# Stores of the feed-forward blocks and the gates issued by the engines that make the data, the residual fetched in four parts, and x ahead of p at the start

## The chip, the cores and the metric

The kernel runs on one core of a Trainium2 chip. A core has five engines that run side by side and wait for each other through semaphores: TensorE (PE, matrix products; its weight loads are listed as PEld), VectorE (DVE), ScalarE (ACT), GpSimd (POOL) and SyncE (SP), which here only issues DMA transfers. The metric is the device time of the whole program in microseconds (us), the median of several runs. Times inside a run are counted from the start of the profiled span.

## What is computed

The reference is one block of an encoder with 1024 tokens of width 1024, in float32:

```
h = x + 0.5 * swiglu(rms_norm(x, g1), Wg1, Wu1, Wd1)      # FFN1, inner width 2816
u = rms_norm(h, g_mix);  z = u @ w_in                     # queries, keys, values, gates
y_a = attention over the 256 best keys of a learned index
y_r = group_norm(chunkwise retention) * silu(rg)
h = h + (sigmoid(ga) * (y_a @ Wa) + sigmoid(gb) * (y_r @ Wb)) @ w_out
h = h + 0.5 * swiglu(rms_norm(h, g2), Wg2, Wu2, Wd2)      # FFN2
h = h + sigmoid(rms_norm(h, g_ple) @ Wpg) * (p @ Wpp)     # per-layer embedding
out = rms_norm(h, g_final)

swiglu(x, Wg, Wu, Wd) = (silu(x @ Wg) * (x @ Wu)) @ Wd
```

## The kernel before

Every float32 operand of a product is split into a high part (a rounded copy, made by ACT at L144 or L401) and a low part (the difference, made by DVE at L146 or L402, or by POOL for some weights), and each product is three matmuls of 128x128 by 128x512 (`split3`).

**Weights.** The class `Weights` holds one list of loads and one list of fills for the whole program. A load takes one of four raw buffers of 512 KB and is a DMA on SP (L155, L172) or a sum or difference made from two raw buffers by POOL (L184, L185, L192, L193). A fill splits a raw buffer into one of four pairs of tiles `wh`, `wl`. `pump` starts a load as soon as a raw buffer is free in the program's order, and a fill as soon as a pair is free. So a load of the next block waits, on SP, for the split that last read its buffer.

**Each FFN** (class `Seven`) uses a form of Strassen's method with seven products in place of eight, in two stages. In `products`, 11 periods (j = 0 to 10) each make the block of 256 inner columns: seven products for the gate matrix, seven for the up matrix (12 matmuls each, `term`, L565), evacuated by ACT (L576, L602) and DVE (L580, L605) into four tiles `h` of 128x512. PE begins to accumulate onto a bank again as soon as ACT has copied it (L576). At the end of a period POOL makes four sums of the four tiles (L627 to L630), and SP stores the seven resulting blocks to DRAM, 256 KB each (`hsp`, L633). Then `down_factors` loads four pieces of the down matrix through SP (L645), POOL forms four differences in place (L646 to L649) and SP stores them (`wsp`, L651): eleven stores a period. In `down`, seven runs of 11 jobs of 12 matmuls (L663) multiply these blocks; each job's raw buffer is filled by two loads of 256 KB, one from `hsp`, one from the down matrix or `wsp`. DVE adds the sums onto the residual `hres` (L672), of which all 16 pieces of 256 KB are fetched before the first run, in FFN1 from x (L796), in FFN2 from `h2spill` (L1548).

**Other stores.** The projection of p (L759) is stored by SP to `ppspill` (L760) while the first norms run; the 24 gate tiles of two halves each are made by ACT (L1036), for the retention gate multiplied by POOL (L1038), and stored by SP (`gspill`, L1039), through two tiles `gt`.

**Order.** The order of PE's instructions is the order of the program text. On the other engines the framework's planner orders the instructions by its own estimate of when each is ready; the engine then works strictly in that order. A DMA on SP whose data or buffer is not ready therefore holds up every DMA behind it.

Of the kernel before, what the change touches and what calls it, by code (L numbers as in the profile page):

```python
# [20 lines left out]
P = 128  # L21
S = 1024
D = 1024
# [254 lines left out]
def hybrid_block_kernel(  # L278
# [27 lines left out]

    LEFT = ["A11", "A12", "S2", "S1", "S3", "S4", "A22"]
    NJ2 = NF // 2  # L310
    hsp, wsp = {}, {}

    def seven_jobs(name, wg, wu, wd):
        hsp[name] = [dram.tile([P, 7, 512], F32, name=f"h{name}{j}") for j in range(NJ2)]
        wsp[name] = [dram.tile([P, 4, 512], F32, name=f"w{name}{j}") for j in range(NJ2)]
        for j in range(NJ2):
            for m, w in (("g", wg), ("u", wu)):
                if (m, j) == ("u", 0):
                    W.early = len(W.fills)
                W.matrix((name, m, j), *(krows(w, 2 * P * j, 2 * P * (j + 1), 4 * q, 4 * q + 4) for q in range(2)))  # L320
        n = W.early
        W.fills[n - 1], W.fills[n] = W.fills[n], W.fills[n - 1]
        for a in LEFT:
            for j in range(NJ2):
                q = LEFT.index(a)
                t = {"S1": 0, "S2": 1, "S3": 2, "A22": 3}.get(a)
                if t is None:
                    f, c = {"A11": (0, 0), "A12": (1, 0), "S4": (1, 512)}[a]
                    wap = krows(wd, c, c + 512, 2 * j + f, 2 * j + f + 1)
                else:  # L330
                    wap = wsp[name][j][:, t:t + 1]
                W.plain((name, a, j), 1, D, False, [(0, 512, hsp[name][j][:, q:q + 1]), (512, D, wap)])
# [150 lines left out]
    class Seven:  # L483
# [66 lines left out]
        def products(self, between):  # L550
# [5 lines left out]
                     "A22": (uh[:, 0:4, b], ul[:, 0:4, b])}  # L556
            left = ExitStack()
            ev = left.enter_context(tc.tile_pool(name="hid", bufs=1))
            g = {0: [ev.tile([P, 512], F32, name=f"g{i}") for i in range(4)]}

            def term(ps, key, start, stop):
                (wh, wl), (bh, bl) = W[key], right[key[1]]
# [42 lines left out]
                return lambda n, t: nc.vector.tensor_tensor(to[n], to[n], t, op=OP.mult)  # L605

            for j in range(NJ2):
                h = g[j % 2]
                gate, up = blocks("g", j, silu(h)), None
                if j == 0:  # L610
                    up = blocks("u", j, times(h))
                    next(gate)
                    next(up)
                    for f in between():
                        f()
                for _ in gate:
                    pass
                if j == 0:
                    self.top.close()
                    sp = self.top.enter_context(tc.tile_pool(name="hid2", bufs=1, side="right"))  # L620
                    g[1] = [sp.tile([P, 512], F32, name=f"g{i}") for i in range(4)]
                for _ in up or blocks("u", j, times(h)):
                    pass
                s1, s2, s4 = (sp.tile([P, 512], F32, name=f"s{i}", tag="s", bufs=8) for i in range(3))
                gp = nc.gpsimd
                h11, h12, h21, h22 = h
                gp.tensor_tensor(s1, h12, h22, op=OP.add)  # L627
                gp.tensor_tensor(s2, s1, h11, op=OP.subtract)
                gp.tensor_tensor(h12, h11, h12, op=OP.subtract)
                gp.tensor_tensor(s4, h21, s2, op=OP.subtract)  # L630
                made = dict(A11=h11, A12=h21, S2=s2, S1=s1, S3=h12, S4=s4, A22=h22)
                for q, n in enumerate(LEFT):
                    nc.sync.dma_start(hsp[self.name][j][:, q], made[n])  # L633
                self.down_factors(sp, j)
            left.close()
            self.top.close()
            self.low.close()

        def down_factors(self, pool, j):

            gp = nc.gpsimd
            b11, b12, b21, b22 = t = [pool.tile([P, 512], F32, name=f"wd{i}", tag="s", bufs=8) for i in range(4)]
            for i in range(4):
                c0 = 512 * (i % 2)
                nc.sync.dma_start(t[i], krows(self.wd, c0, c0 + 512, 2 * j + i // 2, 2 * j + i // 2 + 1)[:, 0])  # L645
            gp.tensor_tensor(b11, b12, b11, op=OP.subtract)  # L646
            gp.tensor_tensor(b12, b22, b12, op=OP.subtract)  # L647
            gp.tensor_tensor(b22, b22, b11, op=OP.subtract)  # L648
            gp.tensor_tensor(b21, b21, b22, op=OP.subtract)  # L649
            for q, d in enumerate((b11, b22, b12, b21)):  # L650
                nc.sync.dma_start(wsp[self.name][j][:, q], d)  # L651

        def down(self, hres, finished, turn, other={}):
            bank_plan(mm=3, m1=1, dn=4)
            sums = [bank(t, "pda") for t in ("mm", "mm", "mm", "m1")]

            def run(a, ps, start, stop, between=None):
                for j in range(NJ2):
                    key = self.name, a, j
                    h, l = (x[:, 0] for x in W[key])  # L660
                    for i in range(4):
                        for n, (x_, y_) in enumerate(split3(h[:, tok(i)], l[:, tok(i)], h[:, 512:D], l[:, 512:D])):
                            nc.tensor.matmul(ps[i], x_, y_, start=start and j == 0 and n == 0,  # L663
                                             stop=stop and j == NJ2 - 1 and n == 2, skip_group_check=True)
                    W.release(key)
                    if between and between.get(j):
                        between[j]()

            def to(ps, t, i):
                for n in range(4):  # L670
                    r = hres[:, 4 * t + n, half(i)]
                    nc.vector.scalar_tensor_tensor(r, ps[n], 0.5, r, op0=OP.mult, op1=OP.add)  # L672

            run("A11", sums, True, False)
            to(sums, 0, 0)
            pc = [bank("dn", "pdc") for _ in range(4)]
            run("A12", pc, True, True)
            to(pc, 0, 0)
            run("S2", sums, False, False)
            to(sums, 0, 1)  # L680
            pc = [bank("dn", "pdc") for _ in range(4)]
            run("S1", pc, True, False)
            to(pc, 1, 1)
            run("S3", sums, False, False)
            to(sums, 1, 1)
            run("S4", pc, False, True)
            to(pc, 0, 1)
            bank_plan(mm=3, m1=1, dn=2, tr=2)
            finished(0)
            finished(1)  # L690

            def turn_and_next(b):
                def go():
                    turn(b)()
                    if b < 2:
                        finished(b + 2)
                return go

            run("A22", sums, False, True, {1 + 2 * b + (b > 1): turn_and_next(b) for b in range(4)} | other)
            to(sums, 1, 0)  # L700
            finished(4)
            finished(5)
# [16 lines left out]
    def load_x(b):  # L719
        nc.sync.dma_start(seven.block(b), x0[tok(b), :])  # L720

    order = [b + 4 * e for b in range(4) for e in range(2)]
    W.limit = 2
    W.load()
    load_p(0)
    seven.open()
    for b in order[:2]:
        load_x(b)
    seven.load_gain()
    W.load()  # L730
    load_p(2)
    for b in order[2:4]:
        load_x(b)
    nc.vector.memset(mhalf, -0.5)
    make_identity(nc, ident)
    W.limit = len(W.loads)
# [17 lines left out]
    def proj_p(b, i):  # L754
        c = slice(P * (b % 2), P * (b % 2) + P)
        th, tl = pt[b & ~1]
        ps = product(("pp", i), b, 2, (lambda k: th[:, k, c], lambda k: tl[:, k, c]))
        t = pk.tile([P, 512], F32, name="ppt", tag="ppt", bufs=2)
        nc.scalar.activation(t, ps, AF.Copy)  # L759
        nc.sync.dma_start(ppspill[:, b, half(i)], t)  # L760

    turns = []
    for i in range(4):
# [27 lines left out]
    ffn1 = ExitStack()  # L791
    hpool = ffn1.enter_context(tc.tile_pool(name="hres1", bufs=1))
    hres = hpool.tile([P, NB, D], F32, name="hres")
    for i in range(2):
        for b in range(NB):
            nc.sync.dma_start(hres[:, b, half(i)], x0[tok(b), half(i)])  # L796
    nc.sync.dma_start(cs, cst)


# [53 lines left out]
            f()  # L853

    finished = normed(mix_norm[0], hres, hspill)
    seven.down(hres, finished, turn, {4: lambda: W.drop(raws)})
    for b in range(2):
        for j in range(2):
            sm_product(2 * b + j, "dn")
# [161 lines left out]
    def gate_half(c, f, i):  # L1021
        box = []

        def piece(k):
# [11 lines left out]
            nc.scalar.activation(t, box[0], AF.Copy if raw else AF.Silu if c == RG else AF.Sigmoid)  # L1036
            if c == RG:
                nc.gpsimd.tensor_tensor(t, t, gnt[:, f:f + 1].to_broadcast([P, 512]), op=OP.mult)  # L1038
            nc.sync.dma_start(gspill[c][:, f, half(i)], t)  # L1039

        return [lambda k=k: piece(k) for k in range(KT)]

# [500 lines left out]
    rpool = late.enter_context(tc.tile_pool(name="res", bufs=1))  # L1543
    hres = rpool.tile([P, NB, D], F32, name="hres2")
    npool = late.enter_context(tc.tile_pool(name="norm2", bufs=1))
    for i in range(2):
        for b in range(NB):
            nc.sync.dma_start(hres[:, b, half(i)], h2spill[:, b, half(i)])  # L1548
    gl = {}

    def ple_gate(b, i=0, parts=1, tag="mm"):
# [7 lines left out]
        return fs + [done]  # L1559

    finished = normed(ple_norm[0], hres)
    seven.down(hres, finished, turn)


    ph = ExitStack()
# [82 lines left out]
```

## Time and profile before

| | us |
|---|---|
| median of three runs (2648.21 to 2649.6) | 2648.36 |
| the profiled execution | 2651.99 |
| its span | 2650.2 |
| PE busy in the span | 2489.3 (94%) |
| DVE, ACT, POOL busy | 1514.1, 1100.8, 899.4 |

The stages by their place in the span: start to 66 us (norm of x, projection of p, first transposes), `products` of FFN1 to 532, `down` of FFN1 to 763, index scores to 925, retention and selection to 1300, attention to 1606, merge and output product to 1874, `products` of FFN2 to 2322, `down` of FFN2 to 2555, and the embedding with the last norm to the end.

To read it: PE's busy time is the sum of the spans of its matmuls; what is left of the span is the time in which PE waited, and the view of waits says for whom. PEclk is the granted clock of TensorE, 1.00 being 2.4 GHz and 0.50 being 1.2 GHz; a mean between the two in a stretch says for which part of it the lower one held. Each other view has its columns named where its rows stand.

### The profile page before, as it was taken

What the parts mean: (1) busy time and instruction counts of PE and PEld (TensorE: products, weight loads), DVE (VectorE), ACT (ScalarE), POOL (GpSimd) and SP (SyncE); (2) the same over time, 40 slices, a digit from 0 to 9 for tenths busy, and PEclk for the clock granted to TensorE, in tenths of its full rate; (3) what the DMA queues carried; (4) which work ended last, traced back from release to release, by engine and by line L of the source; (5) the groups of instructions that cost most, each with busy time, mean ns of one, the idle gap of its engine ahead of it and who ended that gap; (6) DMA issues with size and microseconds to landing.
All of it is one profiled execution on the core that took longest, in us unless ns stands there. A gap on an engine that the chain in (4) does not pass through costs nothing. (4 is left out here: it accounts for less than half of the span.)

```text
span 2650.2 us, 32857 instructions
## 1 busy us (share of the span) xinstructions
PE 2489.3 (94%) x11464; PEld 2030.7 (77%) x11464; DVE 1514.1 (57%) x2640; ACT 1100.8 (42%) x1900; POOL 899.4 (34%) x688
## 2 busy tenths in 40 slices
PE   6999999989999998989999999998999999989998
PEld 5777777768888777767878887787777777768887
DVE  5444444455567879997457664635444444445564
ACT  5333333334355667652235653414323233334452
POOL 5356565410000333343443431004456565410000
PEclk8999999989999999989999999999999999989999
DMA  5244344576640221221221218642244444586632
GB/s 194 92 135 158 130 146 139 172 261 212 192 155 21 84 81 33 68 80 44 86 82 37 82 61 244 183 161 82 94 133 147 130 156 138 174 296 203 196 98 95
DMA packets 272230, 349.36 MB, mean 132 GB/s; under 512 B 22976, under 2 KB 152256, under 8 KB 272064
## 3 DMA queue, kind: packets, MB, share of 16 engines
q1 hardware_dynamic: 272064, 347.27, 41.3%
q8 instruction: 90, 1.47, 0.2%
q14 instruction: 76, 0.62, 0.1%
HBM read 246.00 MB, written 101.19 MB: 131 GB/s over the span
## 5 line engine op out<-in xcount | busy, mean ns | idle before, releaser
L146 DVE TENSOR_TENSOR wl<-wraw,wh 128x1024 fp32r<-128x1024 f32 (+2 forms) x422 | 521.0, 1241 | 542.9 <-ACT wh L144 528.2
L144 ACT ACTIVATE wh<-wraw 128x1024 fp32r<-128x1024 f32 (+1 forms) x466 | 436.5, 938 | 852.1 <-PE pc L565 195.1
L439 PE MATMUL prod<-wh,uh 128*128 128x512 f32 (+1 forms) x648 | 266.6, 411 | 0.2 <-ACT gt L1036 0.2
L439 PE MATMUL prod<-wh,ul 128*128 128x512 f32 (+1 forms) x648 | 257.8, 398 | 0.0
L439 PE MATMUL prod<-wl,uh 128*128 128x512 f32 (+1 forms) x648 | 257.3, 397 | 0.0
L565 PE MATMUL pa<-th,wh 128*128 128x512 f32 x352 | 142.8, 406 | 43.2 <-ACT ev L576 43.2
L1029 PE MATMUL pgate<-uh,wh 128*128 128x512 f32 x384 | 159.2, 415 | 20.9 <-ACT gt L1036 19.8
L663 PE MATMUL pda<-wh 128*128 128x512 f32 x352 | 140.3, 399 | 21.4 <-ACT wh L144 10.7
L465 POOL TENSOR_TENSOR nst<-nst,mhalf 128x1 f32<-128x1 f32 x16 | 8.7, 550 | 443.6 <-DVE nst L464 443.6
L1029 PE MATMUL pgate<-uh,wl 128*128 128x512 f32 x384 | 154.5, 402 | 0.0
L1029 PE MATMUL pgate<-ul,wh 128*128 128x512 f32 x384 | 154.4, 402 | 0.0
L439 PEld LDWEIGHTS prod<-wh,ul 128*128 128x128 f32 x648 | 123.7, 191 | 29.2
L565 PE MATMUL pa<-ul,wh 128*128 128x512 f32 x352 | 141.2, 401 | 4.7 <-DVE ul L402 4.7
L1096 ACT ACTIVATE bias<-bias 128x1024 bf16<-128x1024 bf16 (+3 forms) x132 | 117.3, 890 | 63.0 <-DVE bias L1095 61.7
L146 POOL TENSOR_TENSOR wl<-wraw,wh 128x1024 fp32r<-128x1024 f32 x44 | 109.7, 2496 | 98.5 <-ACT wh L144 97.9
L565 PE MATMUL pa<-th,wl 128*128 128x512 f32 x352 | 142.7, 405 | 0.0
L565 PE MATMUL pa<-uh,wh 128*128 128x512 f32 x352 | 140.6, 399 | 1.8 <-ACT uh L401 1.8
L565 PE MATMUL pa<-tl,wh 128*128 128x512 f32 x352 | 142.0, 403 | 0.0
L663 PE MATMUL pda<-wl,wh 128*128 128x512 f32 x352 | 139.5, 396 | 2.5 <-DVE wl L146 2.5
L565 PE MATMUL pa<-uh,wl 128*128 128x512 f32 x352 | 140.8, 400 | 0.0
L565 PE MATMUL pc<-uh,wl 128*128 128x512 f32 x352 | 139.7, 397 | 0.0
L565 PE MATMUL pc<-ul,wh 128*128 128x512 f32 x352 | 139.6, 396 | 0.0
(274 smaller groups left out, 6008.0 us busy)
## 6 DMA issues: line engine op xcount, KB each, us to landing
wraw<-hf SPq DMA_DIRECT2D x154, 256.0 KB, 3.0
wraw<-in_ffn_w_gate_dram SPq DMA_DIRECT2D x44, 512.0 KB, 5.2
wraw<-in_ffn_w_up_dram SPq DMA_DIRECT2D x44, 512.0 KB, 3.8
hf<-g SPq DMA_DIRECT2D x88, 256.0 KB, 2.3
wd<-in_ffn_w_down_dram SPq DMA_DIRECT2D x88, 256.0 KB, 4.3
wf<-wd SPq DMA_DIRECT2D x88, 256.0 KB, 2.6
wraw<-wf SPq DMA_DIRECT2D x88, 256.0 KB, 3.2
hf<-s SPq DMA_DIRECT2D x66, 256.0 KB, 2.0
```

The costliest lines, as they stand in the source:

```text
L144: self.nc.scalar.activation(h, src, AF.Copy)
L146: eng.tensor_tensor(l, src, h.bitcast(F32), op=OP.subtract)
L439: nc.tensor.matmul(box[0][:, :cols], a, w, start=k == 0 and i == 0, stop=k == nk - 1 and i == 2)
L465: nc.gpsimd.tensor_tensor(st[:, 1:2], st[:, 0:1], mhalf, op=OP.pow)
L565: nc.tensor.matmul(ps, x_, y_, start=start and k == 0 and i == 0, stop=stop and k == 3 and i == 2, skip_group_check=True)
L663: nc.tensor.matmul(ps[i], x_, y_, start=start and j == 0 and n == 0, stop=stop and j == NJ2 - 1 and n == 2, skip_group_check=True)
L1029: nc.tensor.matmul(box[0], a, m, start=k == 0 and j == 0, stop=k == KT - 1 and j == 2)
L1096: nc.scalar.activation(m, m, AF.Copy, accum_out=cnt[:, j:j + 1])
```

## The change

- `products`: the four tiles `h` become one tile of 128x4x512. The seven stores of a period become three, issued by POOL (`nc.gpsimd`): one of 1 MB (`h`, four blocks side by side in DRAM), one of 512 KB (S2 and S1), one of 256 KB (S4). The order of the blocks in DRAM follows (`HID`).
- `down_rows`: the four loads of down-matrix pieces are issued by SP ahead of the up products of the same period, into two tiles of 128x2x2x256; `down_factors` then makes eight differences of 128x256 on POOL and two stores of 512 KB, issued by POOL. The tag `s` has five buffers of 512 KB (it had eight of 256 KB), of which a period takes four.
- `down`: the residual is not fetched before the first run, but in four parts of four pieces, at the fifth job of the runs A11, A12, S2 and S1. A one-column copy on POOL from that job's weights into each piece holds its DMA back until then.
- The stores of the projection of p, and of the gates ga and gb, are issued by ACT; those of the retention gate by POOL.
- At the start p's first load comes first, then one weight load, x's first two blocks and the gain, the second weight load, x's next two blocks, p's second load.

```diff
@@ products
-            g = {0: [ev.tile([P, 512], F32, name=f"g{i}") for i in range(4)]}
+            g = {0: ev.tile([P, 4, 512], F32, name="g0")}
...
+                wd = self.down_rows(sp, j)
                 for _ in up or blocks("u", j, times(h)):
                     pass
-                s1, s2, s4 = (sp.tile([P, 512], F32, name=f"s{i}", tag="s", bufs=8) for i in range(3))
+                sa, sb = (sp.tile([P, 2, 512], F32, name=f"s{i}", tag="s", bufs=5) for i in range(2))
+                s2, s1, s4 = sa[:, 0], sa[:, 1], sb[:, 0]
...
-                for q, n in enumerate(LEFT):
-                    nc.sync.dma_start(hsp[self.name][j][:, q], made[n])
-                self.down_factors(sp, j)
+                to = hsp[self.name][j]
+                gp.dma_start(to[:, 0:4], g[j % 2])
+                gp.dma_start(to[:, 4:6], sa)
+                gp.dma_start(to[:, 6], s4)
+                self.down_factors(wd, j)
@@ down factors
+        def down_rows(self, pool, j):
+            wd = [pool.tile([P, 2, 2, 256], F32, name=f"wd{i}", tag="s", bufs=5) for i in range(2)]
+            for q in range(2):
+                for f in range(2):
+                    rows = krows(self.wd, 0, D, 2 * j + f, 2 * j + f + 1)[:, 0].rearrange("p (i c) -> p i c", i=2)
+                    nc.sync.dma_start(wd[q][:, f], rows[:, :, 256 * q:256 * q + 256])
+            return wd
...
+            for q in range(2):
+                b11, b12, b21, b22 = (wd[q][:, i // 2, i % 2] for i in range(4))
...
+                gp.dma_start(wsp[self.name][j][:, :, 256 * q:256 * q + 256],
+                             wd[q].rearrange("p f i c -> p (f i) c"))
@@ down
+            def fetch(t, i):
+                def go(h):
+                    for b in range(4 * t, 4 * t + 4):
+                        nc.gpsimd.tensor_copy(hres[:, b, 512 * i:512 * i + 1], h[:, 0:1].bitcast(F32))
+                        nc.sync.dma_start(hres[:, b, half(i)], residual(b, i))
+                return go
...
+                    if load and j == 4:
+                        load(h)
...
+            run("A11", sums, True, False, load=fetch(0, 0))
+            run("A12", pc, True, True, load=fetch(0, 1))
+            run("S2", sums, False, False, load=fetch(1, 1))
+            run("S1", pc, True, False, load=fetch(1, 0))
...
-    for i in range(2):
-        for b in range(NB):
-            nc.sync.dma_start(hres[:, b, half(i)], x0[tok(b), half(i)])
@@ projection of p, gates
-        nc.sync.dma_start(ppspill[:, b, half(i)], t)
+        nc.scalar.dma_start(ppspill[:, b, half(i)], t)
...
-            nc.sync.dma_start(gspill[c][:, f, half(i)], t)
+            (nc.gpsimd if c == RG else nc.scalar).dma_start(gspill[c][:, f, half(i)], t)
```

## Rows read from the trace of the kernel before

**Rows 1.** Waits of PE over the whole span: us in total, times, longest us.
```profile
PE pa L565 <- ACT ev L576: 43.2, 18, 4.2
PE pgate L1029 <- ACT gt L1036: 19.8, 8, 4.5
```

**Rows 2.** Timeline of PE: start us, us, what, idle before it and its releaser.
```profile
225.39 0.51 PE L565 MATMUL pa<-th,wh 128*128 128x512 f32 x1 [2.65 <-ACT ev L576]
```

**Rows 3.** Timelines of ACT and DVE in the same period and the half before.
```profile
190.61 1.22 DVE L146 TENSOR_TENSOR wl<-wraw,wh 128x1024 fp32r<-128x1024 f32 x1 [3.31 <-ACT wh L144]
...
209.76 1.23 DVE L146 TENSOR_TENSOR wl<-wraw,wh 128x1024 fp32r<-128x1024 f32 x1 [4.53 <-ACT wh L144]
...
223.21 0.63 ACT L144 ACTIVATE wh<-wraw 128x512 fp32r<-128x512 f32 x1 [7.41 <-DMA wraw<-in_ffn_w_gate_dram]
```

**Rows 4.** Timeline of SP's queue, 180 to 226 us: time of issue, length, transfer, count.
```profile
191.91 0.37 SPq L172 DMA_DIRECT2D wraw<-in_ffn_w_up_dram  x1
...
206.42 0.32 SPq L633 DMA_DIRECT2D hf<-s  x1
...
208.76 0.38 SPq L172 DMA_DIRECT2D wraw<-in_ffn_w_gate_dram  x1
213.42 5.30 SPq L651 DMA_DIRECT2D wf<-wd  x4
218.81 0.39 SPq L172 DMA_DIRECT2D wraw<-in_ffn_w_gate_dram  x1
```

**Rows 5.** Windows of `products`: length, busy us of each engine, PEclk, DMA share, GB/s.
```profile
66.00:532.00 466.00, 440.29 (x1867) 353.80 (x1867) 209.09 (x227) 150.84 (x228) 245.34 (x164) 0.98 0.43 139
...
220.00:260.00 40.00, 37.35 (x155) 29.90 (x154) 18.67 (x20) 13.23 (x20) 21.53 (x15) 0.96 0.42 138
...
1930.00:1970.00 40.00, 39.57 (x159) 31.91 (x160) 17.81 (x20) 11.49 (x17) 22.55 (x15) 0.92 0.43 141
```

**Rows 6.** Windows of the two handovers from `products` to `down`.
```profile
532.00:572.00 40.00, 29.34 (x123) 22.48 (x121) 11.13 (x11) 7.31 (x7) 12.78 (x8) 0.94 0.83 282
572.00:596.00 24.00, 21.73 (x81) 17.37 (x82) 22.81 (x41) 13.07 (x15) 0.00 (x0) 0.81 0.71 230
...
573.00:583.00 10.00, 8.73 (x23) 6.60 (x24) 9.93 (x17) 5.96 (x6) 0.00 (x0) 0.59 0.77 243
...
2322.00:2345.00 23.00, 11.96 (x49) 9.23 (x48) 4.71 (x5) 4.55 (x5) 10.49 (x8) 0.79 0.82 273
...
2343.00:2353.00 10.00, 9.31 (x29) 7.14 (x30) 5.86 (x6) 5.30 (x7) 0.00 (x0) 0.69 0.92 296
```

**Rows 7.** Timelines of SP and PE in the handovers.
```profile
555.49 10.41 SPq L796 DMA_DIRECT2D hres<-in_x_dram  x16
...
566.92 0.33 SPq L155 DMA_DIRECT2D wraw<-in_ffn_w_down_dram  x1
...
573.71 0.80 PE L663 MATMUL pda<-wh 128*128 128x512 f32 x1 [9.37 <-ACT wh L144]
...
2336.68 3.00 SPq L651 DMA_DIRECT2D wf<-wd  x3
```

**Rows 8.** Timeline of ACT at a gate; SP's gate stores: duration ns min/median/max, first and last start us.
```profile
1005.36 1.28 ACT L1036 ACT_TABLE_LOAD   x1
...
L1039 SPq DMA_DIRECT2D gspill<-gt x48: 319/336/1311, 847.2 to 1613.1; - x48
```

**Rows 9.** POOL: one line (ns min/median/max), then groups by shape (busy us, mean ns | idle).
```profile
L649 POOL TENSOR_TENSOR wd<-wd,wd x22: 1262/2151/2261, 133.6 to 2338.1; 128x512 f32<-128x512 f32 x22
...
L1214 POOL TENSOR_TENSOR sl<-sf,sh 128x256 fp32r<-128x256 f32 x28 | 21.7, 777 | 18.0 <-ACT sh L1213 18.0
...
L465 POOL TENSOR_TENSOR nst<-nst,mhalf 128x1 f32<-128x1 f32 x16 | 8.7, 550 | 443.6 <-DVE nst L464 443.6
```

**Rows 10.** The page's DMA issues: count, KB each, median us to landing.
```profile
wf<-wd SPq DMA_DIRECT2D x88, 256.0 KB, 2.6
```

**Rows 11.** Window of the start.
```profile
0.00:66.00 66.00, 45.29 (x204) 35.21 (x204) 34.71 (x48) 36.58 (x65) 34.02 (x35) 0.90 0.57 195
```

More of the change, by code (lines that the diff above doesn't have):

```diff
@@ L302, in tile_job @@
         W.plain(key, nk, n * P, side, [(0, n * P, krows(w, f * P, (f + n) * P, 0, nk))])
+    HID = ["A11", "S3", "A12", "A22", "S2", "S1", "S4"]
     LEFT = ["A11", "A12", "S2", "S1", "S3", "S4", "A22"]
@@ L324, in seven_jobs @@
             for j in range(NJ2):
-                q = LEFT.index(a)
-                t = {"S1": 0, "S2": 1, "S3": 2, "A22": 3}.get(a)
+                q = HID.index(a)
+                t = {"S1": 0, "S3": 1, "A22": 2, "S2": 3}.get(a)
                 if t is None:
@@ L607, in products @@
             for j in range(NJ2):
-                h = g[j % 2]
+                h = [g[j % 2][:, i] for i in range(4)]
                 gate, up = blocks("g", j, silu(h)), None
@@ L620, in products @@
                     sp = self.top.enter_context(tc.tile_pool(name="hid2", bufs=1, side="right"))
-                    g[1] = [sp.tile([P, 512], F32, name=f"g{i}") for i in range(4)]
+                    g[1] = sp.tile([P, 4, 512], F32, name="g1")
+                wd = self.down_rows(sp, j)
                 for _ in up or blocks("u", j, times(h)):
                     pass
-                s1, s2, s4 = (sp.tile([P, 512], F32, name=f"s{i}", tag="s", bufs=8) for i in range(3))
+                sa, sb = (sp.tile([P, 2, 512], F32, name=f"s{i}", tag="s", bufs=5) for i in range(2))
+                s2, s1, s4 = sa[:, 0], sa[:, 1], sb[:, 0]
                 gp = nc.gpsimd
@@ L630, in products @@
                 gp.tensor_tensor(s4, h21, s2, op=OP.subtract)
-                made = dict(A11=h11, A12=h21, S2=s2, S1=s1, S3=h12, S4=s4, A22=h22)
-                for q, n in enumerate(LEFT):
-                    nc.sync.dma_start(hsp[self.name][j][:, q], made[n])
-                self.down_factors(sp, j)
+                to = hsp[self.name][j]
[3 more added lines that the diff above has]
+                self.down_factors(wd, j)
             left.close()
@@ L637, in products @@
             self.low.close()
-        def down_factors(self, pool, j):
-            gp = nc.gpsimd
[L642 to L651, printed above, removed]
@@ L653, in down, with down_factors @@
-        def down(self, hres, finished, turn, other={}):
+        def down_rows(self, pool, j):
[5 more added lines that the diff above has]
+            return wd
+        def down_factors(self, wd, j):
+            gp = nc.gpsimd
+            for q in range(2):
+                b11, b12, b21, b22 = (wd[q][:, i // 2, i % 2] for i in range(4))
+                gp.tensor_tensor(b11, b12, b11, op=OP.subtract)
+                gp.tensor_tensor(b12, b22, b12, op=OP.subtract)
+                gp.tensor_tensor(b22, b22, b11, op=OP.subtract)
+                gp.tensor_tensor(b21, b21, b22, op=OP.subtract)
+                gp.dma_start(wsp[self.name][j][:, :, 256 * q:256 * q + 256],
+                             wd[q].rearrange("p f i c -> p (f i) c"))
@@ L654, in down, with run @@
+        def down(self, hres, residual, finished, turn, other={}):
             bank_plan(mm=3, m1=1, dn=4)
             sums = [bank(t, "pda") for t in ("mm", "mm", "mm", "m1")]
-            def run(a, ps, start, stop, between=None):
+            def fetch(t, i):
[4 more added lines that the diff above has]
+                return go
+            def run(a, ps, start, stop, between=None, load=None):
@@ L672, in to @@
                     nc.vector.scalar_tensor_tensor(r, ps[n], 0.5, r, op0=OP.mult, op1=OP.add)
-            run("A11", sums, True, False)
+            run("A11", sums, True, False, load=fetch(0, 0))
             to(sums, 0, 0)
             pc = [bank("dn", "pdc") for _ in range(4)]
-            run("A12", pc, True, True)
+            run("A12", pc, True, True, load=fetch(0, 1))
             to(pc, 0, 0)
-            run("S2", sums, False, False)
+            run("S2", sums, False, False, load=fetch(1, 1))
             to(sums, 0, 1)
             pc = [bank("dn", "pdc") for _ in range(4)]
-            run("S1", pc, True, False)
+            run("S1", pc, True, False, load=fetch(1, 0))
             to(pc, 1, 1)
@@ L722, in hybrid_block_kernel @@
     order = [b + 4 * e for b in range(4) for e in range(2)]
+    seven.open()
+    load_p(0)
+    W.limit = 1
+    W.load()
+    load_x(order[0])
+    load_x(order[1])
+    seven.load_gain()
     W.limit = 2
     W.load()
[L725 to L731, printed above, removed]
     for b in order[2:4]:
         load_x(b)
+    load_p(2)
     nc.vector.memset(mhalf, -0.5)
@@ L855, in hybrid_block_kernel @@
     finished = normed(mix_norm[0], hres, hspill)
-    seven.down(hres, finished, turn, {4: lambda: W.drop(raws)})
+    seven.down(hres, lambda b, i: x0[tok(b), half(i)], finished, turn, {4: lambda: W.drop(raws)})
     for b in range(2):
@@ L1545, in hybrid_block_kernel @@
     npool = late.enter_context(tc.tile_pool(name="norm2", bufs=1))
-    for i in range(2):
-        for b in range(NB):
-            nc.sync.dma_start(hres[:, b, half(i)], h2spill[:, b, half(i)])
     gl = {}
@@ L1561, in hybrid_block_kernel @@
     finished = normed(ple_norm[0], hres)
-    seven.down(hres, finished, turn)
+    seven.down(hres, lambda b, i: h2spill[:, b, half(i)], finished, turn)
     ph = ExitStack()
```

## The prediction

> **What bounds the kernel now.** I read the page's shares first: PE is busy in 2489.3 of 2650.2 us, so what can be won without taking products away is the 161 us in which it waits, and stretches at the lower clock. Then the waits of PE [rows 1]. The largest is 43.2 us in 18 pieces: a matmul of `products` waits until ACT has copied its bank (L576). ACT is far from full, so the question is what ACT waits for, and the timelines of one period answer it. PE stands for 2.65 us until 225.39 [rows 2]; ACT stood from 215.8 to 223.21, 7.41 us, for the second load of the next gate matrix, and the copy that PE needs is queued behind that split [rows 3]. SP issued this load at 218.81, directly behind the four stores of the down factors, which held SP from 213.42 to 218.72 while POOL made their data [rows 4]. The buffer it loads into had been free since DVE's split of 209.76 ended, 210.99 [rows 3]: the load was 7.8 us late. The other half of the period is the control: there the load at 191.91 follows its split (190.61 + 1.22 = 191.83) at once [rows 3, 4], and no wait of PE follows. The 18 waits lie in 18 different periods of the 22.
>
> The second place is the handover from `products` to `down`. PE is idle 40 - 29.34 = 10.7 and 24 - 21.73 = 2.3 us in FFN1, and 23 - 11.96 = 11.0 us in FFN2 [rows 6]. In FFN1 SP spends 555.49 to 566 on 16 loads of the residual, the next weight load goes out at 566.92, and PE stands 9.37 us until 573.71; in FFN2 SP is held by the last factor stores until 2339.7 [rows 7].
>
> **The change, part by part.**
>
> *Stores of `products` to POOL.* Eleven stores of some 0.33 us and all their waits for POOL leave SP; its queue in the loop keeps loads alone. The late load can go out at about 211, lands before 216, and ACT's split stands ready when a pair of tiles comes free. So the 43.2 us go, and with them what the clock loses after them: in five stretches of 40 us of the two loops (one is shown) the mean granted clock is 0.96, in one 0.92 [rows 5], that is the 1.2 GHz level for 3.2 us and 6.4 us of the stretch, a loss of 5 x 1.6 + 3.2 = 11.2 us. Together 54.4 us. I take 80%: the control half shows that a load in time ends the wait, but the 1 MB store now leaves in one piece beside these loads, and the loads of the down rows sit in SP's queue ahead of the up products, and one of the two buffers they need comes free only when a factor store of the period before has landed. That is 43.5 us off the path.
>
> *What POOL pays.* POOL is busy 245.34 us in 11 periods of FFN1, 22.3 a period [rows 5]. Four differences of 128x512 become eight of 128x256: 8 x 0.777 [rows 9] against some 6.0, +0.3 at most. The five stores have no row: no DMA is issued by POOL in this trace. From below they cost what SP's cost, 0.34 each [rows 8]; a gain is excluded, since POOL issues none now. From above, POOL would be held until the data has landed: 2.6 us for 256 KB [rows 10], for 2.75 MB a period eleven times that, 28.6, or 5.7 a store. I take 1.0: a POOL instruction with almost no data takes 0.55 [rows 9], a store needs no arithmetic on the data, and SP is released long before its data lands. So 22.6 + 5 = 27.6 us of POOL in a period that without waits lasts (466 - 25.7 - 4.8)/11 = 39.6 us [rows 5]: hidden. Behind POOL's stores stand the weight sums of the next matrix; POOL no longer waits for the down rows, which come half a period ahead, and that gives about as much time back.
> A POOL difference beside a DVE split of two SBUF operands takes 2.15 instead of 1.26 us [rows 9], so a store might be stretched by 0.9 us as well, 4.5 us a period, still hidden. The Trainium skill's page "SBUF — State Buffer", section "Who interferes with whom", agrees for arithmetic (a DVE instruction with two SBUF inputs contends with POOL's reads), but infers that writing a DMA's descriptors is not held up by it; by that the 4.5 us would be 0, and the sum is the same either way.
>
> *Handovers.* The stores and waits leave SP here too, and the residual goes out in fours of 256 KB, the first at the fifth job of A11. What can be won: FFN1 12.9 us idle and, after it, 10 us at a mean clock of 0.59, which loses 4.1; FFN2 11.0 and 10 us at 0.69, 3.1 [rows 6]; 31.1 together. I take 65%, 20.2 us: the last period's chain on POOL stays, the DMA engines are 0.82 to 0.92 busy there, and the first quarter of the residual is issued behind POOL's last stores (about 553), lands some 6 us later, and is needed by DVE when A11 ends at 532 + 11 jobs x 12 x 0.227 = 562.
>
> *Gates.* PE's 19.8 us for the gates [rows 1] are not SP's doing: ACT comes late because its own queue is full and a table load of 1.28 us stands before the gate [rows 8]. Nothing is won. 32 stores of 0.34 us [rows 8] come onto ACT, 10.9 us, beside PE's products; behind each stands ACT's next evacuation. I add 1 us (0 to 4). POOL's 16 fall where it is mostly idle.
>
> *Start.* 16 stores of 0.34, 5.4 us, come onto ACT, which is busy 36.6 of 66 us in a chain of short steps [rows 11]; SP, freed of them, loads x earlier; x's second pair goes out half a microsecond sooner. I add 0.7 (-4 to +4).
>
> Sum: -43.5 - 20.2 + 1 + 0.7 = -62.0. The profiled execution took 2651.99 us for its span of 2650.2; the median of the runs is 2648.36, and the difference is taken from that: 2586 us.
>
> **The rivals.**
> 1. *The handovers keep their time*: for it, the DMA engines are 0.82 to 0.92 busy [rows 6], and the same bytes must move; against it, PE stood while SP was held, not while data was on its way. 2648.4 - 43.5 + 1.7 = 2607.
> 2. *SP is held at another place*: the loads of the down rows wait in SP's queue for buffers that POOL's stores free, and the late weight load stands behind them as it stood behind the stores. Five buffers and four taken a period speak for it; that these loads come half a period after those stores speaks against it. The loops keep their 54.4: 2648.4 - 20.2 + 1.7 = 2630.
> 3. *Only issue time is saved*: 242 stores x 0.33 = 80 us of SP's queue, none of it on the path, if each load is late for its own buffer. The 7.8 us between a free buffer and its load speak against it. 2648. The Trainium skill's page "DMA: Bandwidth & Descriptors", section "Issuing engines are not separate DMA queues", speaks for it: starting DMAs from several engines saves only the sequencer's time, usually a small part. The trace differs: what holds SP is the wait for data in an ordered queue.
> 4. *POOL becomes the bound*: with c us for a store a period of POOL is 22.6 + 5c. It reaches PE's 39.6 at c = 3.4, and the whole change loses from c = 4.1 on (22 x (22.6 + 5c - 42.4) = 20). For it: the upper end of 5.7, and two of the stores have rows of 1 KB. At c = 4.5: 22 x 2.7 - 20 = +39, 2688.
>
> **How the numbers follow.** Forecast 55%, rival 1 15%, rival 2 14%, rival 3 6%, rival 4 10%. A measurement of this kernel can tell 0.2%, 5 us, from no change. Faster: 55 + 15 + 14 = 84%; same 6%; slower 10%. Low end: all of 54.4 and 31.1 and the start's 4, 2559, a little below it 2556. High end 2644, which takes in rival 2 and leaves rivals 3 and 4 out.
>
> **What would show it.** Right: no stores in SP's queue in the loops, the gate load within 2 us of its split, PE's wait for L576 under 10 us, no weight load of `down` behind 10 us of residual loads, the gates' wait of some 20 us unchanged. Wrong: POOL stores above 3.4 us, or SP waiting for the buffers of the down rows. The forecast fails if PE's waits in `products` merely change their releaser from ACT's late split to POOL's sums.

## The result, and the profile after

The changed kernel takes 2580.01 us (median of 4 runs, 2576.72 to 2586.53) where the kernel before takes 2648.28 beside it (4 runs, 2644.49 to 2649.6): a ratio of 0.9748, 95% interval 0.9726 to 0.9769. The forecast was 2586, 62 us less than before; 68 came. The profiled execution has a span of 2578.6 us, 71.6 less than before.

First the page's shares of the changed kernel (busy us, share of the span, instructions):

```profile
PE 2471.9 (96%) x11464; PEld 2020.6 (78%) x11464; DVE 1604.5 (62%) x2640; ACT 1104.9 (43%) x1900; POOL 1011.1 (39%) x934
```

PE's idle time fell from 161 us to 106.7, and its busy time by 17.4: the products are the same, but fewer of them run at the lower clock (the mean granted clock of FFN1's loop goes from 0.98 [rows 5] to 0.99, below). Then PE's waits in the changed kernel (us in total, times, longest), against [rows 1]:

```profile
PE pgate L1047 <- ACT gt L1054: 21.7, 9, 5.0
...
PE pda L683 <- ACT wh L144: 4.5, 2, 2.3
```

The 43.2 us for ACT's copy of the products' banks are gone from PE's waits without a rest; the gates' wait is as it was (19.8 before). For ACT's split at the handovers PE waits 4.5 us in two pieces; FFN1's alone had one of 9.37 [rows 7].

Where the time went is told best by stages. Each boundary is the first matmul into a tile: `pa`, `pda`, `pgate`, `pmrg`, the second FFN's `pa` and `pda`; the last stage goes to the end of the span. The experiments below are in the same table (us, each from its one profiled execution; the first stage varies by 5 us, so smaller differences carry nothing):

| kernel | start | products 1 | down 1, index | retention, attention | merge | products 2 | down 2, end |
|---|---|---|---|---|---|---|---|
| before | 67.6 | 464.9 | 305.4 | 768.4 | 247.5 | 467.8 | 328.6 |
| after | 66.7 | 442.1 | 292.3 | 770.5 | 247.2 | 440.0 | 319.8 |
| e1_stores_only | 66.0 | 438.4 | 295.4 | 768.0 | 246.1 | 441.4 | 320.0 |
| e2_residual_only | 69.1 | 468.6 | 293.0 | 767.2 | 249.5 | 467.8 | 327.4 |
| e3_issued_by_sp | 64.4 | 507.5 | 294.9 | 769.5 | 249.4 | 503.5 | 321.0 |
| e4_rows_late | 64.6 | 461.6 | 295.8 | 771.6 | 248.2 | 459.4 | 328.7 |
| e5_small_back | 68.4 | 439.7 | 290.8 | 767.4 | 247.3 | 440.9 | 321.0 |
| e6_pool_2_chain | 65.1 | 458.8 | 292.4 | 773.3 | 248.3 | 475.3 | 321.0 |
| e7_pool_2_early | 64.6 | 441.3 | 293.8 | 769.0 | 251.0 | 440.5 | 320.1 |
| e8_raw_gates | 64.5 | 441.9 | 292.3 | 768.3 | 247.7 | 440.9 | 319.5 |

Two loops of products give 22.8 and 27.8 us, two handovers 13.1 and 8.8; the rest is within 2.1.

Windows of the changed kernel that answer to [rows 5, 6]: first the loop of FFN1, 40 us of it and 40 of FFN2's, then the two handovers (length, busy us of PE, PEld, DVE, ACT, POOL, then PEclk, DMA share, GB/s):

```profile
66.70:508.80 442.10, 435.25 (x1869) 350.78 (x1870) 251.57 (x227) 150.56 (x225) 295.40 (x266) 0.99 0.45 151
200.00:240.00 40.00, 39.75 (x172) 31.87 (x171) 24.18 (x20) 13.34 (x20) 28.41 (x26) 1.00 0.45 152
1900.00:1940.00 40.00, 39.78 (x172) 31.89 (x171) 24.40 (x21) 13.34 (x20) 27.96 (x25) 1.00 0.45 152
508.80:548.80 40.00, 36.90 (x156) 29.87 (x155) 28.56 (x47) 16.54 (x18) 11.77 (x15) 0.96 0.82 265
2258.80:2281.80 23.00, 20.10 (x80) 15.85 (x79) 8.54 (x8) 7.71 (x8) 11.13 (x11) 0.93 0.80 283
```

PE is nearly without a gap in the loops, 0.2 us idle in each 40, at a mean granted clock of 0.99 or 1.00. At the handovers its idle time is 3.1 us (it was 10.7) and 2.9 (11.0), while the DMA engines are about as busy as before, 0.82 and 0.80 (0.83 and 0.82 in [rows 6]): the bytes still move, and PE no longer stands for them. Two columns have grown: POOL from 245.34 to 295.40, and DVE from 209.09 to 251.57, although DVE does nothing new. That is the surprise of this case, taken up below.

SP's queue in one period (against [rows 4]), then the two splits that its last gate load stands between, DVE's that frees the buffer and ACT's that needs the data:

```profile
189.02 0.37 SPq L172 DMA_DIRECT2D wraw<-in_ffn_w_up_dram  x1
189.49 1.21 SPq L648 DMA_DIRECT2D wd<-in_ffn_w_down_dram  x2
202.64 0.38 SPq L172 DMA_DIRECT2D wraw<-in_ffn_w_gate_dram  x1
203.12 1.21 SPq L648 DMA_DIRECT2D wd<-in_ffn_w_down_dram  x2
211.48 0.38 SPq L172 DMA_DIRECT2D wraw<-in_ffn_w_gate_dram  x1
```

```profile
207.22 4.17 DVE L146 TENSOR_TENSOR wl<-wraw,wh 128x1024 fp32r<-128x1024 f32 x1 [1.15 <-ACT wh L144]
```

```profile
215.32 0.63 ACT L144 ACTIVATE wh<-wraw 128x512 fp32r<-128x512 f32 x1 [1.20 <-DMA wraw<-in_ffn_w_gate_dram]
```

Only loads are left in the queue. The gate load goes out at 211.48, 0.09 us after DVE's split ends at 207.22 + 4.17 = 211.39; before it came 7.8 us late. ACT still waits for it, but 1.20 us and not 7.41.

POOL's new work in the changed kernel: its stores by line (busy us, mean ns, idle).

```profile
L660 POOL DMA_DIRECT2D wf<-wd x44 | 32.3, 735 | 8.2 <-POOL wd L659 7.1 <-issue 1.0
L635 POOL DMA_DIRECT2D hf<-g x22 | 12.7, 576 | 0.0
...
L637 POOL DMA_DIRECT2D hf<-s x22 | 12.0, 547 | 0.0
```

A store of `products` holds POOL for 0.55 to 0.74 us in the mean, and not in proportion to its size: the 1 MB store of L635 takes 576 ns, the 256 KB store of L637 547, and the longest, 735, are the 512 KB stores of L660 with rows of 1 KB.

### The profile page after: what moved, and what is told of

It is laid out like the page before. It is cut to its first block, busy times and chain, and to the rows that moved or that the text cites. A ratio compares the mean times of both kernels' runs of the same rounds, so it can differ in the third digit from the quotient of the medians.

```text
span 2578.6 us, 32601 instructions
## 1 busy us (share of the span) xinstructions
PE 2471.9 (96%) x11464; PEld 2020.6 (78%) x11464; DVE 1604.5 (62%) x2640; ACT 1104.9 (43%) x1900; POOL 1011.1 (39%) x934
## 4 chain that ended last, share of the span: by engine, by line
PE 73%; DVE 12%; issue 5%; ACT 4%; POOL 3%; DMA 3%; SPq 0%; ACTq 0%; POOLq 0%; DVEq 0%
PE pa L566 18%; PE pc L566 13%; PE prod L440 11%; PE pda L683 9%; PE pdc L683 7%; PE pgate L1047 6%; PE pmrg L396 4%; DVE bias L1113 3%; DVE wl L146 1%; ACT bias L1114 1%; PE ppt L1366 1%; PE psc L396 1%; PE ppv L1377 1%; PE plg L396 1%; ACT wh L144 1%
## 5 line engine op out<-in xcount | busy, mean ns | idle before, releaser
L146 DVE TENSOR_TENSOR wl<-wraw,wh 128x1024 fp32r<-128x1024 f32 (+2 forms) x422 | 610.1, 1447 | 419.9 <-ACT wh L144 418.6
L1047 PE MATMUL pgate<-uh,wh 128*128 128x512 f32 x384 | 158.7, 413 | 22.7 <-ACT gt L1054 21.7
L1114 ACT ACTIVATE bias<-bias 128x1024 bf16<-128x1024 bf16 (+3 forms) x132 | 117.0, 888 | 59.5 <-DVE bias L1113 55.7
L566 PE MATMUL pc<-uh,wh 128*128 128x512 f32 x352 | 139.4, 396 | 0.0
L440 PEld LDWEIGHTS prod<-wh,uh 128*128 128x128 f32 x648 | 124.4, 192 | 18.7 <-ACT gt L1054 0.4
L440 PEld LDWEIGHTS prod<-wl,uh 128*128 128x128 f32 x648 | 124.3, 192 | 18.4
```

The costliest lines, as they stand in the source:

```text
L146: eng.tensor_tensor(l, src, h.bitcast(F32), op=OP.subtract)
L440: nc.tensor.matmul(box[0][:, :cols], a, w, start=k == 0 and i == 0, stop=k == nk - 1 and i == 2)
L566: nc.tensor.matmul(ps, x_, y_, start=start and k == 0 and i == 0, stop=stop and k == 3 and i == 2, skip_group_check=True)
L1047: nc.tensor.matmul(box[0], a, m, start=k == 0 and j == 0, stop=k == KT - 1 and j == 2)
L1114: nc.scalar.activation(m, m, AF.Copy, accum_out=cnt[:, j:j + 1])
```

## The experiments

The first four kernels ran beside a run of the kernel before of 2651.81 us, the last four beside one of 2649.23.

**e1_stores_only.** The kernel before with the edits of `products` alone: merged stores by POOL, down rows loaded ahead. The residual, gates, pp and start are as before.

```diff
  (changed kernel, with these taken back)
-            run("A11", sums, True, False, load=fetch(0, 0))
+            run("A11", sums, True, False)
...
-        nc.scalar.dma_start(ppspill[:, b, half(i)], t)
+        nc.sync.dma_start(ppspill[:, b, half(i)], t)
```

> The kernel before with the edits of products alone (three stores of hidden blocks and two of factor blocks a period issued by POOL, down rows loaded ahead of the up products); residual, gates, p and start as before. Theory (SP's ordered queue, held by stores that wait for POOL, made the weight loads late): the 43 us of PE's wait for L576 and the clock lost behind it go, and with the stores also a part of the handovers, since SP is held there by 16 residual loads and by stores: 2648 - 50 - 10 = 2588, 2580 to 2598. Rival (the gain needs the residual's four parts as well, because the handovers hold half of it): 2605 or more.

Measured: 2580.25 us, ratio 0.9735 (0.9712 to 0.9757), the whole gain. The handovers gain 10.0 and 8.6 us with the residual still fetched in one run. SP's queue at FFN1's handover in this kernel:

```profile
518.95 0.32 SPq L155 DMA_DIRECT2D wraw<-hf  x1
...
520.45 0.43 SPq L155 DMA_DIRECT2D wraw<-in_ffn_w_down_dram  x1
520.92 10.29 SPq L806 DMA_DIRECT2D hres<-in_x_dram  x15
```

The residual holds the queue for 10.29 us as it did [rows 7], but SP, with no stores to wait for, comes to it earlier and with one more buffer of `down` loaded (eleven, before ten). The first load of `down` behind it goes out at 532.24, 27.8 us after `down` has begun; in the kernel before it was 566.92, 34.4 us after. PE waits 4.5 us in two pieces at the two handovers, as in the changed kernel.

**e2_residual_only.** The kernel before with the residual in four parts, and nothing else.

```diff
-    for i in range(2):
-        for b in range(NB):
-            nc.sync.dma_start(hres[:, b, half(i)], x0[tok(b), half(i)])
...
+            run("A11", sums, True, False, load=fetch(0, 0))
```

> The kernel before with the residual fetched in four parts, and nothing else. Theory: the loops keep their waits, only the handover of FFN1 gains, where 10 us of residual loads stood before a weight load: 2648 - 14 = 2634, 2626 to 2642; PE's wait for L576 stays at 40 to 46 us. Rival (the handovers are bound by the bytes, DMA share 0.82 to 0.92): 2645 to 2650.

Measured: 2636.7 us, ratio 0.9948 (0.9932 to 0.9964), as the theory said, with 45.2 us of PE's wait for L576 left. By stages the gain is FFN1's handover alone, 12.4 us; FFN2's gives 1.2. (The profiled execution took 2644.36 us, 7.7 above the median; the stages add up to 7.6 us of gain, the medians to 15.1, and where the rest lies this profile can't show.) In FFN2 SP is still held by the last factor stores:

```profile
2329.97 3.00 SPq L651 DMA_DIRECT2D wf<-wd  x3
```

```profile
PE pda L673 <- DMA pp<-ppspill: 10.4, 1, 10.4
```

This wait lies at FFN2's handover (the kernel before has it there with 10.6 us, the changed kernel not at all); the load that the view names stands in SP's queue behind these stores.

So FFN1's handover is won by either edit, FFN2's by the stores' alone, and the two don't add.

**e3_issued_by_sp.** The changed kernel with its five merged stores issued by SP: same tiles, sizes, order in the text.

```diff
-                gp.dma_start(to[:, 0:4], g[j % 2])
+                nc.sync.dma_start(to[:, 0:4], g[j % 2])
...
-                gp.dma_start(wsp[self.name][j][:, :, 256 * q:256 * q + 256],
+                nc.sync.dma_start(wsp[self.name][j][:, :, 256 * q:256 * q + 256],
```

> The changed kernel with the five stores of a period issued by SP again, as merged as in the change, down rows still loaded ahead. Theory (the issuing queue decides): SP is held until POOL has made the factor blocks, the gate load behind it is late again, 2580 + 30 to 50 = 2610 to 2630, with PE's wait for L576 (L577 in this text) back at 25 to 45 us. Rival (fewer, larger stores and rows loaded ahead are what shortens the loops): 2578 to 2586.

Measured: 2714.35 us, ratio 1.0239 (1.0221 to 1.0257), 134 us above the changed kernel and worse than either theory had it. PE's, ACT's and SP's waits in this kernel, one fence each, then a piece of SP's queue:

```profile
PE pa L566 <- ACT ev L577: 92.5, 18, 5.8
```

```profile
ACT wh L144 <- DMA wraw<-in_ffn_w_gate_dram: 178.2, 18, 10.5
```

```profile
SPq L636 <- POOL s L631: 171.3, 21, 8.4
SPq L660 <- POOL wd L659: 135.1, 43, 4.0
```

```profile
180.70 3.69 SPq L660 DMA_DIRECT2D wf<-wd  x2
184.50 0.57 SPq L172 DMA_DIRECT2D wraw<-in_ffn_w_gate_dram  x1
```

The chain of the kernel before, longer: SP stands at a store whose data POOL has not made, the gate load goes out behind it (184.50), ACT's split waits 10.17 us for it, and the copy that PE wants stands behind the split. With SP as the issuer, merging and loading ahead win nothing; that doesn't make them worthless once POOL issues, as e4 shows for the loading. This form is 63 us worse than the kernel before beside it (2651.81), with fewer stores: PE's wait for ACT's copy is 92.5 us where it was 43.2, and the loops are 78.3 us longer. Why its queue is held longer than the old one stays open.

**e4_rows_late.** The changed kernel with the down rows loaded after the up products, as before; all stores stay with POOL.

```diff
-                wd = self.down_rows(sp, j)
...
-                self.down_factors(wd, j)
+                self.down_factors(self.down_rows(sp, j), j)
```

> The changed kernel with the down rows loaded where they were loaded before, behind the sums of the period. Theory: POOL waits some 4 us a period for the rows, as before, which is covered; SP only issues: 2578 to 2588. Rival (loading the rows ahead is what freed the queue): 2600 or more.

Measured: 2630.18 us, ratio 0.9921 (0.99 to 0.9941). My theory missed by over 40 us, and for a reason that neither side named. PE's waits, then one of the twenty in PE's timeline, and POOL's and DVE's timelines ahead of it:

```profile
PE pa L566 <- DVE ev L581: 35.0, 20, 1.9
...
PE pda L682 <- ACT wh L144: 15.7, 2, 10.2
```

```profile
214.19 0.50 PE L566 MATMUL pa<-uh,wh 128*128 128x512 f32 x1 [1.74 <-DVE ev L581]
```

```profile
206.83 1.45 POOL L655 TENSOR_TENSOR wd<-wd 128x256 f32<-128x256 f32 x2
...
211.03 1.42 POOL L658 TENSOR_TENSOR wd<-wd 128x256 f32<-128x256 f32 x2
212.40 1.47 POOL L659 DMA_DIRECT2D wf<-wd  x2
```

```profile
207.88 5.66 DVE L146 TENSOR_TENSOR wl<-wraw,wh 128x1024 fp32r<-128x1024 f32 x1 [1.16 <-ACT wh L144]
213.46 0.67 DVE L581 TENSOR_TENSOR ev<-ev,pa 128x512 f32<-128x512 f32 x1
```

With the rows late, POOL does its eight differences in pairs and without a gap. DVE's split of two SBUF operands, which takes 1.22 and 1.23 us in [rows 3], starts at 207.88 and ends at 213.54: 1.09 us after POOL's last difference ended (212.45), as if it had begun only then. The evacuation L581 stands behind it, and PE waits 1.74 us until 214.19. The rival's number came, but not by its reason, a queue that isn't free: SP's queue has only loads in this stretch, and the second of the two gate loads here goes out at 213.60, when the held split has ended.

```profile
203.29 10.68 SPq L172 DMA_DIRECT2D wraw<-in_ffn_w_gate_dram  x2
```

In the changed kernel the same split is let in sooner. POOL's differences stand there in another order, and between the following two it pauses for 0.08 us:

```profile
209.57 0.73 POOL L658 TENSOR_TENSOR wd<-wd 128x256 f32<-128x256 f32 x1
210.38 1.60 POOL L659 TENSOR_TENSOR wd<-wd 128x256 f32<-128x256 f32 x1
```

The split of 207.22 ends at 211.39, again 1.09 us after a POOL operation (L658, at 210.30), and L659 takes 1.60 us where the others take 0.73. It is so in 11 of the changed kernel's 22 periods; in e4 the split lasts through all the differences in 20. So the releaser changed from ACT to DVE, not to POOL's sums as my prediction had it. This was read from the trace; e6 and e7 test it.

**e5_small_back.** The changed kernel with the gates' and pp's stores back on SP, and the old order of the start.

```diff
-            (nc.gpsimd if c == RG else nc.scalar).dma_start(gspill[c][:, f, half(i)], t)
+            nc.sync.dma_start(gspill[c][:, f, half(i)], t)
...
```

> The changed kernel with three small edits undone: the stores of the gates and of the retention's pp blocks go back to SP's queue, and the order of the start is that of the kernel before. Theory (these edits are worth nothing): 2577 to 2584 us, and TensorE's wait for the gates' evacuation (line of gt) stays near 21 us. Rival (the gates' stores off SP, or x ahead at the start, carry part of the gain): over 2588.

Measured: 2579.02 us, ratio 0.9733 (0.9712 to 0.9754); the gates' wait is 19.9 us. These three edits give and cost nothing that can be measured.

**e6_pool_2_chain and e7_pool_2_early.** Two more adds of 128x512 on POOL in each period, result unused; in e6 behind the stores, in the chain; in e7 ahead of POOL's sums, where it stood idle.

```diff
  (e6)
                 self.down_factors(wd, j)
+                for _ in range(2):
+                    gp.tensor_tensor(sb[:, 1], s4, s4, op=OP.add)
  (e7)
+                for _ in range(2):
+                    gp.tensor_tensor(sb[:, 1], h11, h11, op=OP.add)
                 gp.tensor_tensor(s1, h12, h22, op=OP.add)
```

> The changed kernel with two extra adds of 128x512 (about 1.3 us each, result unused) on GpSimd in every period of the products, put right behind the stores, into the chain of GpSimd's operations that VectorE's two-operand split was seen to last through. Theory A (VectorE's split can't end until GpSimd's chain has a gap): VectorE's 128x1024 split lasts 2 us longer in each period, TensorE waits for the evacuation behind it (line L581) 1.5 to 2.5 us in each of 40 periods: 2630 to 2670 us. Theory B (GpSimd only costs when it is full): GpSimd holds 26.5 + 2.6 = 29.1 of the 39.6 us of a period, so nothing changes: 2577 to 2588 us.

> The changed kernel with the same two extra adds of 128x512 on GpSimd in every period, but ahead of its sums, where GpSimd stood idle for 7.75 us. Theory A (it is the unbroken chain that holds VectorE): GpSimd's sums begin at most 1 us later, 2577 to 2595 us, far below the kernel with the adds in the chain. Theory B (GpSimd full or not): 2577 to 2588. Theory C (any further work of GpSimd slows VectorE in proportion): as with the adds in the chain, within 10 us of that kernel's time.

Measured: e6 2633.78 us, ratio 0.9929 (0.9905 to 0.9953); e7 2583.04, ratio 0.9747 (0.9721 to 0.9772). The same work costs 54 us in one place and nothing that can be told in the other. POOL has room in both, so it isn't POOL being full (theory B), nor its amount of work (C). Theory A is left, and only in part: its price was right and the way to it was not (I had 40 waits of 2 us, and there are 8 of 5), and e7, further down, shows that a chain without a gap does not always hold the split. PE's waits, then POOL, DVE and PE in one such period of e6:

```profile
PE pa L566 <- DVE ev L581: 39.6, 8, 5.0
```

```profile
319.87 1.07 POOL L640 TENSOR_TENSOR s<-s 128x512 f32<-128x512 f32 x1
320.91 1.29 POOL L192 TENSOR_TENSOR wraw<-wraw 128x512 f32<-128x512 f32 x1
322.17 1.03 POOL L640 TENSOR_TENSOR s<-s 128x512 f32<-128x512 f32 x1
...
327.29 1.39 POOL L661 TENSOR_TENSOR wd<-wd 128x256 f32<-128x256 f32 x2
328.64 1.43 POOL L662 DMA_DIRECT2D wf<-wd  x2
```

```profile
320.89 8.88 DVE L146 TENSOR_TENSOR wl<-wraw,wh 128x1024 fp32r<-128x1024 f32 x1 [0.85 <-ACT wh L144]
329.69 0.68 DVE L581 TENSOR_TENSOR ev<-ev,pa 128x512 f32<-128x512 f32 x1
```

```profile
330.42 0.80 PE L566 MATMUL pa<-uh,wh 128*128 128x512 f32 x1 [4.95 <-DVE ev L581]
```

DVE's split takes 8.88 us and again ends 1.09 us after POOL's last difference (327.29 + 1.39 = 328.68). And the first matmul after the wait takes 0.80 us, not 0.39. The two loops are 52 us longer than the changed kernel's: PE is idle 36.7 us more in them and busy 15.3 us more for the same matmuls, at mean granted clocks of 0.98 and 0.96 against 0.99 and 1.00. In nine other periods of e6 DVE got in halfway, and then a pair of POOL's differences took 2.44 us, not 1.43:

```profile
204.22 3.43 DVE L146 TENSOR_TENSOR wl<-wraw,wh 128x1024 fp32r<-128x1024 f32 x1 [0.86 <-ACT wh L144]
```

```profile
206.49 2.44 POOL L658 TENSOR_TENSOR wd<-wd 128x256 f32<-128x256 f32 x2
208.90 1.43 POOL L659 TENSOR_TENSOR wd<-wd 128x256 f32<-128x256 f32 x2
```

In e7 the eight differences stand in pairs without a gap, as in e4, but the split begins ahead of them, and it ends 1.08 us after the one operation that it began beside (L192, until 204.03):

```profile
203.99 2.42 POOL L658 TENSOR_TENSOR wd<-wd 128x256 f32<-128x256 f32 x2
```

```profile
203.38 1.73 DVE L146 TENSOR_TENSOR wl<-wraw,wh 128x1024 fp32r<-128x1024 f32 x1 [1.55 <-ACT wh L144]
```

In 17 periods of e7 it begins ahead of them and takes 1.4 to 1.8 us. In two others the split begins 1.0 us behind the start of the differences, as in e4, and lasts 5.68 and 5.67 us; PE has two waits behind it, 3.5 us together. So it also matters where in the chain the split begins. What decides which of the two yields, the runs don't tell.

**e8_raw_gates.** The changed kernel with ga and gb always stored without their sigmoid, which the merge then applies.

```diff
-            raw_gates[c, f, i] = raw = bool(at)
+            raw_gates[c, f, i] = raw = c != RG
```

> The changed kernel with the two gates that are stored in halves stored without their sigmoid, which is applied when they are read back in the merge. It is to show what TensorE's 21.7 us of waits at the gates are. Theory (the table loads of ScalarE between sigmoid and the copies make these waits): under 6 us of them left and 2560 to 2570 us. Rival (ScalarE pays the same again in the merge, or the waits come from something else): 2575 to 2590 us.

Measured: 2581.35 us, ratio 0.9739 (0.9717 to 0.9761); the gates' wait stays at 22.4 us. So it isn't table loads. In the changed kernel the gates have one, and 17.8 of the 21.7 us lie from 1000 to 1200 us, where no table is loaded; in e8 this stretch has 18.4 us. The load (count, busy us, mean ns):

```profile
L1054 ACT ACT_TABLE_LOAD x1 | 1.3, 1283 | 0.0
```

What ACT did ahead of a late copy in the changed kernel, and PE behind it:

```profile
1044.17 0.83 ACT L1114 ACTIVATE bias<-bias 128x768 bf16<-128x768 bf16 x1
...
1045.98 1.05 ACT L144 ACTIVATE wh<-wraw 128x1024 fp32r<-128x1024 f32 x1
1046.92 0.58 ACT L1054 ACTIVATE gt<-pgate 128x512 f32<-128x512 f32 x1
```

```profile
1047.56 0.80 PE L1047 MATMUL pgate<-uh,wh 128*128 128x512 f32 x1 [4.96 <-ACT gt L1054]
```

The counting passes of the index (L1114) and a split stand ahead of the gate's copy, which waits its turn (one wait of the nine, the longest). No kernel here beats the changed one by more than can be told; the cheapest form of it is e1.

## Why the prediction was right, point by point

- **Loops.** The wait [rows 1], its cause (a load behind stores that wait for POOL) and the cure were right: no stores in SP's queue, the load 0.09 us behind its split, the wait gone with the clock's dips. The term was too small: 43.5 forecast, 50.6 measured by stages, of 54.4 to be had. e1 shows that the edits of `products` do it, e3 that they don't without the issuing queue, e4 that the queue without the rows ahead gives 21.6 us in all (2630.18 against 2651.81). Whether the merging of the stores has a part in it, no run tells.
- **The rows ahead.** I counted this only as a risk (rival 2), and let POOL gain "about as much time" by it. It is worth 50 us: e4 without it gives back 19.5 and 19.4 us in the loops and 12.4 at the handovers. That the change held this edit was luck as far as the prediction goes: without it the time would have been 2630, within the range, but by a wait that no part of the prediction has. The step that was missing is DVE: beside a run of POOL operations without a gap, a DVE operation of two SBUF operands can last until the run ends. For the handovers' 12.4 this wasn't followed up.
- **Handovers.** -20.2 forecast, -21.9 measured. The size was right, the parts were not: the stores' move alone gives 18.6 of it (e1), because SP then comes to the residual earlier and to the loads of `down` behind it in time, and the four parts of the residual add nothing to that which can be told from noise.
- **POOL.** 1.0 us a store was forecast between 0.34 and 5.7; it is 0.55 to 0.74, and the period holds 295.40 / 11 = 26.9 us of POOL (27.6 forecast), far from PE's 39.6. Rival 4 needed 4.1 us. The 1 MB store takes 571 to 579 ns in all 22 cases, in 21 of them beside a split of DVE, so it isn't stretched by 0.9 us as I had allowed for.
- **Gates and start.** +1 and +0.7 forecast, +2.1 and -0.9 by stages, nothing by e5. The cause that I gave for the gates' wait was half wrong: not the table load (e8); ACT's full queue, yes, by the timeline of one wait.
- **Rivals.** 1 fell with the handovers' gain, 2 with SP's queue (the second pair of rows goes out at 203.12 and the gate load 8.4 us later is on time), 3 with the total. The Trainium skill's page "DMA: Bandwidth & Descriptors", section "Issuing engines are not separate DMA queues", says that issuing from several engines saves only the sequencer's time. Here the trace disagrees: five stores a period moved from SP to POOL are 134 us (e3 against the changed kernel), where the sequencer's time would be 22 x 5 x 0.33 = 36 us, an estimate from SP's stores [rows 8], and off the path. What is saved is waiting in an ordered queue.

## What to carry to other kernels

A DMA that waits for data belongs in the queue of the engine that makes the data: here that freed a queue of loads to run ahead, and the stores cost POOL 0.55 to 0.74 us each, off the path. Before two edits at one place are both credited, do each alone; here one gave all of it. When work moves to POOL, don't only add up its busy time: look at what it runs without a gap, and at which DVE operations with two SBUF operands begin inside that stretch.

## What was not expected of the hardware

A DVE operation that reads two SBUF operands can be held by a whole run of POOL operations, not by one. The 128x1024 split, 1.22 and 1.23 us in [rows 3], took 4.17 us beside POOL's chain in the changed kernel, 5.66 in e4 and 8.88 in e6; in the last two it ended 1.09 us after the chain's last difference, in the changed kernel 1.09 us after the difference behind which POOL pauses for 0.08 us. A chain without a pause doesn't always do it: in nine periods of e6 and 17 of e7 DVE got in between. POOL's stores don't hold it: the 5.66 and the 8.88 us end while POOL issues the stores behind the chain. The Trainium skill's page "SBUF — State Buffer", section "Who interferes with whom", has DVE with two SBUF inputs contend with POOL's reads, for ports that are an exclusive lock, and lets issue order decide who blocks. These traces agree that it blocks, but the split stayed blocked through operations that POOL began after it.
